# Hybrid conv block on one core: c's row on GpSimd's queue, wide constants for the clock, two unsplit chunks in the lead, and the second half's sum in front of the last chunk

## The chip, the cores and the metric

The kernel runs on one core of one Trainium2 chip. The metric is the device time of one execution in microseconds (us). TensorE is PE in the profile, VectorE is DVE, ScalarE is ACT, GpSimd is POOL and SyncE is SP. All arithmetic is float32; a matmul operand marked fp32r passes through TensorE once, and the kernel reaches float32 accuracy by splitting each operand into a high and a low fp32r part.

## The reference, cut to what matters

```python
def reference(x, c, ...):            # x (1, 1024, 1024), c (1, 1024), all float32
    mod = silu(c) @ w_ada + b_ada    # 6 * 1024 values
    sh1, sc1, g1, sh2, sc2, g2 = split(mod, 6)
    h = rms_norm(x, norm_mix_g) * (1 + sc1) + sh1
    proj = h @ w_in                  # 7 * 1024 columns
    b_s, c_s, v_s, v_c, gl_c, gate_br = split(proj)
    y_a = (b_s * causal_dwconv(c_s * v_s, 3 taps)) @ w_short_out
    u = causal_dwconv(v_c * sigmoid(gl_c), 31 taps) + bias
    y_b = silu(layer_norm(u)) @ w_conf_out
    g_a, g_b = split(sigmoid(gate_br))
    x = x + g1 * ((g_a * y_a + g_b * y_b) @ w_o)
    h2 = rms_norm(x, norm_ffn_g) * (1 + sc2) + sh2
    a, b = split(h2 @ w_ffn_in)
    x = x + g2 * ((silu(a) * b) @ w_ffn_out)
    return rms_norm(x, final_norm_g)
```

## The kernel before

Everything lies transposed: channels on the 128 partitions, positions along the row. The 1024 channels are eight chunks, numbered k = 0 to 7 here as in the code (the words "chunk 8" of the change's title mean k = 7). The 1024 positions are two halves of 512, h = 0 and h = 1. A tile framework fixes the order of the instructions on each engine when the program is built; every engine, and every DMA queue, then goes through its list in order and waits where an operand is not there. `tc.issue_after(ins)` puts what follows behind the instruction `ins` in that planning.

The change is in the lead, the first 5% of the program, up to the second half's first products. Its steps, with lines of the kernel before:

- **c's row.** `c` (4 KB, one partition) is loaded into `crow`, tile name `diff` (L540, issued by ACT), then `vecs` (184 KB of small vectors, L541, issued by ACT). A dummy Silu (L543) loads ACT's table, `crow` goes through Silu (L550), a second dummy (L424) loads the table with the reciprocal root. Two matmuls `cb` (L556) with one row of ones spread silu(c) over all partitions, and ACT copies them to SBUF as `cs` (L562).
- **Clock matmuls.** `keep_clock` (L529 to L536) issues matmuls that nobody reads, 128x128 in float32, chained to the work around them: 7 ahead of `cb`, 2 after each of five additions of squares, 6 on ones after the sum, 10 that read the tile `rx0r`. The tuple `CLOCK` holds these counts.
- **The norm of the first half.** `squares_x` (L488 on ACT, L492 on DVE) squares the eight chunks and adds them, six into one tile and two into another. `norm_start` sums over the partitions with two matmuls `ss` (L502) and takes the reciprocal root on ACT (`rx0r`, L399). `rstd_square` squares that (`rx0t`, L412). `rstd_negative` (L417, L418) is one Newton step on DVE, the second instruction written in place over `rx0r`.
- **The modulation.** For each k two blocks of `w_ada` (512 KB each, tile `ada`) are loaded by SP and multiplied and summed with `cs` on DVE (L329). `affine` (L335) makes the scale, `modulate` (L428 on DVE, L432 or L436 and L440 on ACT, L437 on DVE) makes the operand.
- **The lead's products.** `row_blocks` runs over k and, for each k, over seven output tiles `lead`. For k below `WHOLE` (3) weight and operand go to TensorE unsplit, as float32 (L344, two records for each matmul in the profile). From there on both are split: the weight by ACT (L220, `wh`) and DVE (L221, `wl`), the operand by L436 and L437, and each output tile takes three fp32r matmuls (L348, L349, L351).
- **The norm of the second half.** At k = 5 eight loads of `xT` (256 KB each, L595) are issued, at k = 6 their squares are summed and `ss` and the reciprocal root `rx1` begin, at k = 7 the Newton step ends. Then `row_blocks` runs again for h = 1, beginning with the kept weights of chunks 5, 6 and 7.

Behind the lead come the rest of the input projection, the convolutions, the output projections and the feed-forward part; the change does not touch their code.

Of the kernel before, what the change touches and what calls it, by code (L numbers as in the profile page):

```python
# [44 lines left out]
KC = D // P  # L45
# [4 lines left out]
EPS = 1e-6  # L50
# [3 lines left out]
V_GMIX, V_GFFN, V_GFIN, V_LNG, V_LNB, V_CB = (8 * i for i in range(6))  # L54
# [9 lines left out]


LEAD = 7
WHOLE = 3

CLOCK = (7, 2, 6, 10)


KEPT = 3
SECOND = [*range(KC - KEPT, KC), *range(KC - KEPT)]


SQ_LAST = 2


X1_AT = 5
# [40 lines left out]
def block_kernel(ctx: ExitStack, tc: tile.TileContext, x0, xT, c, vecs, ada, w_first, w_plain, w_duals,  # L122
                 w_short, w_conf, w_o, w_fi, w_fo, w_last, outT):
    nc = tc.nc
# [13 lines left out]
    cp = pool("const", 1)  # L138
# [16 lines left out]
    def ps2_tile(name):  # L155
        return ps2p.tile([P, H], F32, tag="ps2", name=name)
# [30 lines left out]
    ng = cp.tile([P, V_LNG], F32, name="ng")  # L187
# [152 lines left out]
    def mm3(outs, wsl, w, xs, first, last, again=False):  # L340

        if w[1] is None:
            for ps, x in zip(outs, xs):
                mm3.ins = nc.tensor.matmul(ps, w[0][:, wsl], x, start=first, stop=last).ins  # L344
            return
        wh, wl = w[0][:, wsl], w[1][:, wsl]
        for ps, (xh, xl) in zip(outs, xs):
            nc.tensor.matmul(ps, wh, xh, start=first, stop=False, skip_group_check=again)  # L348
# [60 lines left out]
    def rstd_square(begun):  # L409

        ss, eps, r, q, _ = begun
        nc.scalar.activation(q, r, AF.Square, scale=0.5 ** 0.5)  # L412
        return ss, r, q

    def rstd_negative(ss, r, q):

        nc.vector.scalar_tensor_tensor(out=q, in0=ss, scalar=EPS, in1=q, op0=ALU.add, op1=ALU.mult)  # L417
        nc.vector.scalar_tensor_tensor(out=r, in0=q, scalar=1.5, in1=r, op0=ALU.subtract, op1=ALU.mult)  # L418
        return r

    def load_rsqrt(ins):

        with tc.issue_after(ins):
            nc.scalar.activation(cp.tile([P, 1], F32, name="rs"), ones[:, :1], AF.Abs_reciprocal_sqrt)  # L424

    def modulate(src, r, scale, shift, name, begun=None):

# [36 lines left out]
    def row_blocks(act, n, name, ops, unit, joined=2):  # L464


        outs = [(ps_tile if o < 6 else ps2_tile)(f"{name}{o}") for o in range(n)]
        ops = list(ops)
        for k in range(KC):
            if k == len(ops):  # L470
                xs = act(k)
                ops.append((unit(k), xs))
            if KC - joined <= k < KC - 1:
                continue
            for o in range(n):
                for kk in range(KC - joined, KC) if k == KC - 1 else (k,):
                    w, xs = ops[kk]
                    mm3([outs[o]], slice(o * P, o * P + P), w, [xs], kk == 0, kk == KC - 1)
        return outs


    x = {}

    def squares_x(src, acc=None, clock=0):

        for t in src:
            sq = g_tile("sq")
            act = nc.scalar.activation(sq, t, AF.Square, scale=1.0 / 32.0)  # L488
            if acc is None:
                acc = sq  # L490
            else:
                add = nc.vector.tensor_tensor(acc, acc, sq, ALU.add)  # L492
                if clock:
                    keep_clock(keep_clock.ins, clock, sq)
        squares_x.ins = act.ins, add.ins
        return acc

    def norm_start(acc, name, n=H, tile_of=g_tile, ss_tile=ps_tile):
        ss = ss_tile("ss")
        acc = acc if isinstance(acc, list) else [acc]  # L500
        for t in acc:
            norm_start.ins = nc.tensor.matmul(ss[:, :n], ones, t, start=t is acc[0], stop=t is acc[-1]).ins  # L502
        return rstd_start(ss, eps1, name, n, tile_of)
# [22 lines left out]
        nc.scalar.activation(sig, ps, AF.Sigmoid)  # L526
        nc.scalar.dma_start(gate_dram[b, j][:, halves[h]], sig)

    def keep_clock(ins, n, src=None):  # L529

        t = ps2_tile("clock")[:, :P]
        src = ones if src is None else src[:, :P]
        for _ in range(n):
            with tc.issue_after(ins) if ins else ExitStack():
                ins = nc.tensor.matmul(t, ones, src, start=True, stop=True).ins
# [4 lines left out]
    nc.scalar.dma_start(crow, c)  # L540
    nc.scalar.dma_start(vec, vecs)  # L541
    nc.vector.tensor_scalar(ng, vec[:, :V_LNG], -1.0, None, ALU.mult)
    nc.scalar.activation(cp.tile([P, 1], F32, name="si"), ones[:, :1], AF.Silu)  # L543
    xin = {}
    for k in range(0, KC, 2):
        t = uc_tile("x0", T)
        nc.sync.dma_start(t, x0[k // 2])
        xin[k], xin[k + 1] = (t[:, s] for s in halves)
    keep_clock(None, CLOCK[0])
    silu = nc.scalar.activation(crow, crow, AF.Silu)  # L550
    load_rsqrt(silu.ins)
    cb = []
    for s in halves:
        cb.append(ps_tile("cb"))
        with tc.issue_after(keep_clock.ins):
            mm = nc.tensor.matmul(cb[-1], ones[:1], crow[:, s], start=True, stop=True)  # L556
    keep_clock.ins = mm.ins
    acc = squares_x([xin[k] for k in range(KC - SQ_LAST)], clock=CLOCK[1])
    acc = [acc, squares_x([xin[k] for k in range(KC - SQ_LAST, KC)])]
    with tc.issue_after(squares_x.ins[0]):  # L560
        for s, t in zip(halves, cb):
            nc.scalar.copy(cs[:, s], t)  # L562
    with tc.issue_after(keep_clock.ins):
        rx_0 = norm_start(acc, "rx0")
    keep_clock(norm_start.ins, CLOCK[2])
    keep_clock(keep_clock.ins, CLOCK[3], rx_0[2])
    rx_0 = rstd_square(rx_0)

    def lead_w(k):
# [4 lines left out]
            kept.append(w)  # L574
        return w

    def act_x(k, h):
        nonlocal rx_0, rx_1
        if h == 0:
            with ExitStack() as after:  # L580
                after.enter_context(tc.issue_after(modulate.ins[0] if k else squares_x.ins[1]))
                for i in range(2 * k, 2 * k + 2):
                    modulation(i, ucp.tile([P, T + CK - 1], F32, tag="uc", name="ada")[:, :D])
            affine(naff1, k, 8, ng, V_GMIX)
            if k == 0:
                rx_0 = rstd_negative(*rx_0)
            x[k, 0] = s_tile(f"x{k}0")
        whole = h == 0 and k < WHOLE
        hT[k][h] = modulate(x[k, h], rx_1 if h else rx_0, naff1[:, k : k + 1], modc(k),
                            None if whole else f"h{k}{h}", None if h else xin[k])  # L590
        if h == 0:
            if k == X1_AT:
                for i in range(KC):
                    x[i, 1] = s_tile(f"x{i}1")
                    nc.sync.dma_start(x[i, 1], xT[i, :, halves[1]])  # L595
            elif k == X1_AT + 1:
                with tc.issue_after(modulate.ins[2]):
                    rx_1 = squares_x([x[i, 1] for i in range(KC)])
                with tc.issue_after(mm3.ins), tc.issue_after(modulate.ins[1]):
                    rx_1 = rstd_square(norm_start(rx_1, "rx1", ss_tile=ps2_tile))  # L600
            elif k == KC - 1:
                with tc.issue_after(modulate.ins[2]):
                    rx_1 = rstd_negative(*rx_1)
            if whole:
                return x[k, 0]
        elif k < WHOLE:
            hT[k][0] = split(x[k, 0], hl_tile, f"h{k}0")
        return hT[k][h]
# [605 lines left out]
    ss = ps_tile("ss")  # L1214
# [54 lines left out]
    n = 2 * GROUP * P  # L1269
# [184 lines left out]
```

## Time and profile before

| | |
|---|---|
| median of 3 runs | 1476.24 us (1476.24 to 1478.43) |
| the profiled execution, its own time | 1477.93 us |
| its span, first to last instruction | 1476.2 us |
| PE busy | 1462.0 us (99% of the span) |
| DVE busy | 1177.7 us (80%) |
| ACT busy | 617.0 us (42%) |
| POOL busy | 513.3 us (35%) |

The profile is that of one execution, whose own time is 1.7 us above the median of the runs and above its span. Busy times are averages over the whole program; in the first 20 us TensorE mostly runs the clock matmuls, so its busy share says nothing there, and times have to be read from the order of the rows. A row of the timeline gives start, duration, engine, line, operation, tile written and tiles read, and in brackets the idle time of that engine ahead of it with what ended it.

### The profile page before, as it was taken

The numbers are of one execution on the slowest core, as the hardware profiler recorded it, in microseconds if no ns is written. First come the engines' busy times: TensorE is split into PE (matmuls) and PEld (weight loads), VectorE is DVE, ScalarE is ACT, GpSimd is POOL, SyncE is SP. The second block draws the span as 40 slices with busy tenths as digits, with TensorE's granted clock in tenths as the row PEclk, the third lists the DMA queues.
The fourth block names the chain that finished last, engine by engine and source line by source line (L and its number), as shares of the span: only waits on it lengthen the run. The fifth ranks groups of instructions, "written<-read, shape, count | busy, mean of one in ns | idle before, by whom it ended". The sixth has DMA issues, their size and how long they took to land.

```text
span 1476.2 us, 17809 instructions
## 1 busy us (share of the span) xinstructions
PE 1462.0 (99%) x6475; PEld 1200.4 (81%) x6475; DVE 1177.7 (80%) x1623; ACT 617.0 (42%) x896; POOL 513.3 (35%) x459
## 2 busy tenths in 40 slices
PE   9999999999999999999999999999999999999997
PEld 5888888888888888878888878888888888888887
DVE  7999888887998969999687699777777765677755
ACT  4653433333333335555235465444444443222235
POOL 0036677767877771111022001101111015535005
PEclk9999999999999999999999999999999999999999
DMA  8522213222222267376685337655455449988403
GB/s 342 188 64 72 100 58 128 72 86 100 91 67 86 82 219 285 105 237 213 200 311 172 117 100 235 209 176 168 150 192 166 146 149 371 357 287 276 156 1 115
DMA packets 83274, 245.36 MB, mean 166 GB/s; under 512 B 9585, under 2 KB 11761, under 8 KB 83186
## 3 DMA queue, kind: packets, MB, share of 16 engines
q1 hardware_dynamic: 42352, 136.01, 27.6%
q0 software_dynamic: 36944, 95.44, 19.6%
q10 hardware_dynamic: 3890, 12.78, 2.3%
q8 instruction: 51, 0.84, 0.2%
q14 instruction: 37, 0.30, 0.1%
HBM read 181.79 MB, written 62.39 MB: 165 GB/s over the span
## 4 chain that ended last, share of the span: by engine, by line
PE 91%; DVE 6%; DMA 1%; issue 1%; ACT 1%; POOL 0%; POOLq 0%; DVEq 0%; ACTq 0%
PE bank L351 11%; PE bank L348 11%; PE bank L349 11%; PE x L351 7%; PE x L348 7%; PE x L349 7%; PE z L349 4%; PE z L348 4%; PE z L351 4%; PE y L349 3%; PE y L348 3%; PE y L351 3%; PE yb L351 2%; PE yb L348 2%; PE yb L349 2%; PE mix L349 2%
## 5 line engine op out<-in xcount | busy, mean ns | idle before, releaser
L220 ACT CAST wh<-raw 128x1024 fp32r<-128x1024 f32 (+2 forms) x254 | 256.3, 1011 | 485.2 <-PE bank L349 133.6
L221 POOL TENSOR_TENSOR wl<-raw,wh 128x1024 fp32r<-128x1024 f32 x84 | 204.5, 2444 | 81.8 <-ACT wh L220 81.8
L221 DVE TENSOR_TENSOR wl<-raw,wh 128x1024 fp32r<-128x1024 f32 (+2 forms) x170 | 195.0, 1147 | 47.5 <-ACT wh L220 46.2
L838 DVE SCALAR_TENSOR_TENSOR c<-diff,vec,c 128x512 f32<-128x512 f32 x232 | 171.0, 753 | 4.4
L1170 POOL DMA_DIRECT2D hid<-stage x71 | 37.8, 533 | 347.0 <-DVE stage L389 341.0
L348 PE MATMUL bank<-th,wh 128*128 128x512 f32 x288 | 112.0, 389 | 0.0
L349 PE MATMUL bank<-tl,wh 128*128 128x512 f32 x288 | 112.0, 389 | 0.0
L351 PE MATMUL bank<-th,wl 128*128 128x512 f32 x288 | 112.0, 389 | 0.0
L838 DVE SCALAR_TENSOR_TENSOR c<-u,wsum,c 128x512 f32<-128x512 f32 x112 | 84.3, 753 | 2.6
L240 POOL TENSOR_TENSOR raw<-raw 128x1024 f32<-128x1024 f32 x12 | 29.2, 2430 | 130.4 <-DVE wl L221 92.8
L388 ACT CAST stage<-g 128x512 fp32r<-128x512 f32 x62 | 38.4, 622 | 65.9 <-DMA hid<-stage 35.4
L351 PEld LDWEIGHTS bank<-th,wl 128*128 128x128 f32 x288 | 54.1, 188 | 11.3
L349 PEld LDWEIGHTS bank<-tl,wh 128*128 128x128 f32 x288 | 54.1, 188 | 11.2
L348 PEld LDWEIGHTS bank<-th,wh 128*128 128x128 f32 x288 | 54.1, 188 | 11.2
L389 DVE TENSOR_TENSOR stage<-g,stage 128x512 fp32r<-128x512 f32 x62 | 42.4, 689 | 25.3 <-ACT stage L388 25.3
L1196 POOL DMA_DIRECT2D th<-hid x71 | 38.0, 535 | 53.2 <-PE x L351 31.9
L348 PE MATMUL x<-th,wh 128*128 128x512 f32 x144 | 56.1, 390 | 0.0
L349 PE MATMUL x<-tl,wh 128*128 128x512 f32 x144 | 56.0, 389 | 0.0
L351 PE MATMUL x<-th,wl 128*128 128x512 f32 x144 | 56.0, 389 | 0.0
L348 PE MATMUL yb<-zsh,wh 128*128 128x512 f32 x128 | 49.8, 389 | 0.0
L349 PE MATMUL yb<-zsl,wh 128*128 128x512 f32 x128 | 49.8, 389 | 0.0
L351 PE MATMUL yb<-zsh,wl 128*128 128x512 f32 x128 | 49.8, 389 | 0.0
(798 smaller groups left out, 4211.3 us busy)
## 6 DMA issues: line engine op xcount, KB each, us to landing
hid<-stage POOLq DMA_DIRECT2D x71, 512.0 KB, 4.4
raw<-in_w_fi SPq DMA_DIRECT2D x51, 512.0 KB, 3.7
raw<-in_w_duals SPq DMA_DIRECT2D x48, 512.0 KB, 3.5
th<-hid POOLq DMA_DIRECT2D x71, 256.0 KB, 5.7
tl<-hid POOLq DMA_DIRECT2D x71, 256.0 KB, 5.7
ada<-in_ada SPq DMA_DIRECT2D x24, 512.0 KB, 5.9
raw<-in_ada SPq DMA_DIRECT2D x24, 512.0 KB, 4.6
raw<-in_w_fo SPq DMA_DIRECT2D x24, 384.0 KB, 5.7
```

Source lines behind the costliest of these rows:

```text
L220: hi = nc.scalar.copy(wh, raw)
L221: lo = lo_engine.tensor_tensor(wl, raw, f32(wh), ALU.subtract)
L240: eng.tensor_tensor(a["s1"], a["21"], a["22"], ALU.add)
L348: nc.tensor.matmul(ps, wh, xh, start=first, stop=False, skip_group_check=again)
L349: nc.tensor.matmul(ps, wh, xl, start=False, stop=False, skip_group_check=again)
L351: mm3.ins = nc.tensor.matmul(ps, wl, xh, start=False, stop=last, skip_group_check=again).ins
L388: t_split.act = nc.scalar.copy(hi, src).ins
L389: t_split.ins = nc.vector.tensor_tensor(lo, src, f32(hi), ALU.subtract).ins
L838: tap.ins = nc.vector.scalar_tensor_tensor(out=out, in0=src[:, s : s + H], scalar=wt, in1=acc, op0=ALU.mult, op1=ALU.add).ins
L1170: nc.gpsimd.dma_start(hid_dram[key], s)
L1196: nc.gpsimd.dma_start(t, hid_dram[key][:, s])
```

## The change

- `WHOLE` goes from 3 to 2: chunk k = 2 of the first half is split like the later ones.
- `c` is loaded by GpSimd's queue instead of ACT's. ACT's first instructions are then the load of `vecs`, the dummy Silu, Silu of c's row and the second table.
- `keep_clock` can issue wide matmuls: 128x512, fp32r, on a new tile `ones_r` filled by DVE. There are 6 wide ones ahead of `cb`; one small and one wide after each of five additions; 6 wide after the sum; one small on the new tile `newton` and 3 wide; one small on `rx0r` and 2 wide.
- The first Newton instruction writes `newton` and no longer `rx0t`; the second still writes `rx0r`, which no clock matmul reads ahead of it any more.
- The squares of the first half take buffers of the large pool (58) instead of one with 6.
- The first half of `cs` is copied by DVE ahead of the additions, the second by ACT behind the squares. The scaled gains `ng` are made after that copy.
- For k = 7 the modulation's DVE work stands behind the last addition of the second half's squares, and every product of k = 7 stands behind that half's `ss` matmul.

In the program as it is built, this changes the order on the engines in the lead only (up to about 75 us of the profile before); behind it the lists of all engines hold the same instructions in the same order, but for one place in the numbering of GpSimd's DMAs.

```diff
-WHOLE = 3
+WHOLE = 2
-CLOCK = (7, 2, 6, 10)
+CLOCK = (6, range(1, 6), 6, (3, 2))
...
-    def rstd_negative(ss, r, q):
+    def rstd_negative(ss, r, q, t=None):
-        nc.vector.scalar_tensor_tensor(out=q, in0=ss, scalar=EPS, in1=q, op0=ALU.add, op1=ALU.mult)
-        nc.vector.scalar_tensor_tensor(out=r, in0=q, scalar=1.5, in1=r, op0=ALU.subtract, op1=ALU.mult)
+        t = q if t is None else t
+        nc.vector.scalar_tensor_tensor(out=t, in0=ss, scalar=EPS, in1=q, op0=ALU.add, op1=ALU.mult)
+        nc.vector.scalar_tensor_tensor(out=r, in0=t, scalar=1.5, in1=r, op0=ALU.subtract, op1=ALU.mult)
...
         for k in range(KC):
             if k == len(ops):
                 xs = act(k)
                 ops.append((unit(k), xs))
+                first = getattr(act, "first", None)
...
-                    mm3([outs[o]], slice(o * P, o * P + P), w, [xs], kk == 0, kk == KC - 1)
+                    with tc.issue_after(first) if first and k == KC - 1 else ExitStack():
+                        mm3([outs[o]], slice(o * P, o * P + P), w, [xs], kk == 0, kk == KC - 1)
...
-                if clock:
-                    keep_clock(keep_clock.ins, clock, sq)
+                if i in clock:
+                    keep_clock(keep_clock.ins, 1, sq)
+                    keep_clock(keep_clock.ins, 1, wide=True)
...
-    def keep_clock(ins, n, src=None):
-        t = ps2_tile("clock")[:, :P]
-        src = ones if src is None else src[:, :P]
+    def keep_clock(ins, n, src=None, wide=False):
+        t = ps2_tile("clock")
+        lhs, src = (ones_r[:, :P], ones_r) if wide else (ones, ones if src is None else src[:, :P])
         for _ in range(n):
             with tc.issue_after(ins) if ins else ExitStack():
-                ins = nc.tensor.matmul(t, ones, src, start=True, stop=True).ins
+                ins = nc.tensor.matmul(t[:, : src.shape[-1]], lhs, src, start=True, stop=True).ins
...
-    nc.scalar.dma_start(crow, c)
+    nc.gpsimd.dma_start(crow, c)
     nc.scalar.dma_start(vec, vecs)
-    nc.vector.tensor_scalar(ng, vec[:, :V_LNG], -1.0, None, ALU.mult)
...
-    keep_clock(None, CLOCK[0])
+    ones_r = s_tile("ones_r", F32R)
+    nc.vector.memset(f32(ones_r), 1.0)
+    keep_clock(None, CLOCK[0], wide=True)
...
-    acc = squares_x([xin[k] for k in range(KC - SQ_LAST)], clock=CLOCK[1])
-    acc = [acc, squares_x([xin[k] for k in range(KC - SQ_LAST, KC)])]
+    copy = nc.vector.tensor_copy(cs[:, halves[0]], cb[0])
+    with tc.issue_after(copy.ins), tc.issue_after(load_rsqrt.ins):
+        nc.vector.tensor_scalar(ng, vec[:, :V_LNG], -1.0, None, ALU.mult)
+        acc = squares_x([xin[k] for k in range(KC - SQ_LAST)], clock=CLOCK[1], tile_of=s_tile)
+        acc = [acc, squares_x([xin[k] for k in range(KC - SQ_LAST, KC)], tile_of=s_tile)]
     with tc.issue_after(squares_x.ins[0]):
-        for s, t in zip(halves, cb):
-            nc.scalar.copy(cs[:, s], t)
+        nc.scalar.copy(cs[:, halves[1]], cb[1])
     with tc.issue_after(keep_clock.ins):
         rx_0 = norm_start(acc, "rx0")
-    keep_clock(norm_start.ins, CLOCK[2])
-    keep_clock(keep_clock.ins, CLOCK[3], rx_0[2])
+    keep_clock(norm_start.ins, CLOCK[2], wide=True)
...
-                after.enter_context(tc.issue_after(modulate.ins[0] if k else squares_x.ins[1]))
+                after.enter_context(tc.issue_after(squares_x.ins[1] if k in (0, X1_AT + 2) else modulate.ins[0]))
...
             if k == 0:
-                rx_0 = rstd_negative(*rx_0)
+                t = s_tile("newton")
+                rx_0 = rstd_negative(*rx_0, t)
+                for src, n in zip((t, rx_0), CLOCK[3]):
+                    keep_clock(keep_clock.ins, 1, src)
+                    keep_clock(keep_clock.ins, n, wide=True)
...
-                with tc.issue_after(modulate.ins[2]):
+                with tc.issue_after(modulate.ins[2]), tc.issue_after(modulate.ins[1]):
                     rx_1 = squares_x([x[i, 1] for i in range(KC)])
                 with tc.issue_after(mm3.ins), tc.issue_after(modulate.ins[1]):
                     rx_1 = rstd_square(norm_start(rx_1, "rx1", ss_tile=ps2_tile))
+                act_x.first = norm_start.ins
...
-        lead = row_blocks(lambda i: act_x(SECOND[i] if h else i, h), LEAD, "lead", ops, again_w if h else lead_w, 1 + h)
+        lead = row_blocks(act_x if h == 0 else lambda i: act_x(SECOND[i], 1), LEAD, "lead", ops,
+                          again_w if h else lead_w, 1 + h)
```

More of the change, by code (lines that the diff above doesn't have):

```diff
@@ L423, in load_rsqrt @@
         with tc.issue_after(ins):
-            nc.scalar.activation(cp.tile([P, 1], F32, name="rs"), ones[:, :1], AF.Abs_reciprocal_sqrt)
+            act = nc.scalar.activation(cp.tile([P, 1], F32, name="rs"), ones[:, :1], AF.Abs_reciprocal_sqrt)
+        load_rsqrt.ins = act.ins
     def modulate(src, r, scale, shift, name, begun=None):
@@ L467, in row_blocks @@
         outs = [(ps_tile if o < 6 else ps2_tile)(f"{name}{o}") for o in range(n)]
-        ops = list(ops)
+        ops, first = list(ops), None
         for k in range(KC):
@@ L477, in row_blocks, with squares_x @@
                     w, xs = ops[kk]
-                    mm3([outs[o]], slice(o * P, o * P + P), w, [xs], kk == 0, kk == KC - 1)
+                    with tc.issue_after(first) if first and k == KC - 1 else ExitStack():
+                        mm3([outs[o]], slice(o * P, o * P + P), w, [xs], kk == 0, kk == KC - 1)
         return outs
     x = {}
-    def squares_x(src, acc=None, clock=0):
-        for t in src:
-            sq = g_tile("sq")
+    def squares_x(src, acc=None, clock=(), tile_of=g_tile):
+        for i, t in enumerate(src):
+            sq = tile_of("sq")
             act = nc.scalar.activation(sq, t, AF.Square, scale=1.0 / 32.0)
@@ L555, in block_kernel @@
         with tc.issue_after(keep_clock.ins):
-            mm = nc.tensor.matmul(cb[-1], ones[:1], crow[:, s], start=True, stop=True)
-    keep_clock.ins = mm.ins
-    acc = squares_x([xin[k] for k in range(KC - SQ_LAST)], clock=CLOCK[1])
-    acc = [acc, squares_x([xin[k] for k in range(KC - SQ_LAST, KC)])]
+            keep_clock.ins = nc.tensor.matmul(cb[-1], ones[:1], crow[:, s], start=True, stop=True).ins
+    copy = nc.vector.tensor_copy(cs[:, halves[0]], cb[0])
[3 more added lines that the diff above has]
+        acc = [acc, squares_x([xin[k] for k in range(KC - SQ_LAST, KC)], tile_of=s_tile)]
     with tc.issue_after(squares_x.ins[0]):
-        for s, t in zip(halves, cb):
-            nc.scalar.copy(cs[:, s], t)
+        nc.scalar.copy(cs[:, halves[1]], cb[1])
     with tc.issue_after(keep_clock.ins):
         rx_0 = norm_start(acc, "rx0")
-    keep_clock(norm_start.ins, CLOCK[2])
-    keep_clock(keep_clock.ins, CLOCK[3], rx_0[2])
+    keep_clock(norm_start.ins, CLOCK[2], wide=True)
     rx_0 = rstd_square(rx_0)
@@ L575, in lead_w, with act_x @@
         return w
-    def act_x(k, h):
+    def act_x(k, h=0):
         nonlocal rx_0, rx_1
```

## The prediction, as it was put on record

> **What bounds the kernel now.** I read the page first, then the chain of work that ended last in order of time, then the timelines of PE, DVE and ACT for the first 75 us.
>
> ```profile
> span 1476.2 us, 17809 instructions
> PE 1462.0 (99%) x6475; PEld 1200.4 (81%) x6475; DVE 1177.7 (80%) x1623; ACT 617.0 (42%) x896; POOL 513.3 (35%) x459
> ```
>
> ```profile
> 1.06 3.35 PE clock L535 x14
> 4.42 3.71 PE cb L556 x4
> 8.12 4.34 PE clock L535 x20
> 12.47 1.72 PE ss L502 x4
> 14.19 3.58 PE clock L535 x32
> 17.79 0.70 DVE rx0r L418
> 18.52 0.76 DVE x L428
> 19.31 0.73 ACT x L432
> 20.08 18.29 PE lead L344 x42
> ```
>
> TensorE is busy all the time; its longest pause is the one ahead of the first real product at 20.08, from the end of the clock matmuls (14.19 + 3.58 = 17.77) on, 2.3 us. From there on it is fed, so whatever brings the first product forward, or takes matmuls out of the stream, shortens the whole; behind the lead the instruction lists are the same and the shift is carried to the end. Ahead of 20.08 the chain runs over clock matmuls, that is, TensorE's own queue sets the time of the sums that DVE and ACT wait for.
>
> The rows also show TensorE slow and then fast: the same 128x128 matmul record takes 4.34 / 20 = 0.217 us from 8.12 on and 3.58 / 32 = 0.112 us from 14.19 on. The change is between those two stretches; I take 0.217 as cold and 0.112 as warm.
>
> **The change part by part.** The sum is made against the profiled execution, 1477.93 us with a span of 1476.2, and then taken off the median, 1476.24, which lies 1.7 us lower; the three runs reach from 1476.24 to 1478.43. About 0.2% (2.95 us) is what a measurement of this kernel can tell from no change.
>
> *c's row.*
>
> ```profile
> 0.74 0.51 ACTq L540 DMA_DIRECT2D diff<-in_c  x1
> 0.74 0.30 POOL L173 MEMSET fill<- 128x248 f32 x1 [0.29 <-POOLq L1443]
> ...
> 3.09 1.04 ACT L550 ACTIVATE diff<-diff 1x1024 f32<-1x1024 f32 x1
> ```
>
> c's row had landed by 3.09, when Silu began behind the load of its table. Without the issue of 0.51 on ACT's queue the table comes 0.5 earlier and Silu could start at 2.6. But c now goes behind GpSimd's fill, issued at 0.74 + 0.30 = 1.05, through a queue whose first landing the trace of before does not show. Three rows bound it, by the DMAs' times to landing: ACT's gate stores, GpSimd's `hid` stores, and `vec`, which shared the engines with x's loads as c will.
>
> ```profile
> DMA to landing us min/median/max: 2.0/2.0/2.9
> ```
>
> ```profile
> DMA to landing us min/median/max: 2.9/4.4/8.3
> ```
>
> ```profile
> vec<-in_vecs ACTq DMA_DIRECT2D x1, 184.0 KB, 5.0
> ```
>
> So c lands between 1.05 + 2.0 = 3.05 and 1.05 + 5.0 = 6.05. I take 3.1: the first row is of 256 KB, the second of 512 KB, and c has 4 KB. Silu then ends at 4.1 to 4.2, as before. The six wide clock matmuls wait for DVE to fill `ones_r` (about 1.5) and take, cold, twice the fp32r pitch of 0.228 us (a split chunk below: 4.78 for 21), 6 x 0.456 = 2.7, so they end at 4.2. `cb` starts at 4.3, where it was 4.42: 0.1 gained, 3 us lost at the other bound.
>
> *Clock matmuls up to `ss`.* `cb` takes 3.71 and ends at 8.0. Before, 20 records took 4.34. Now there are five pairs, each two cold small records and a cold wide one: 5 x (2 x 0.217 + 0.456) = 4.5. The additions that release them come in time: DVE's copy of `cs` follows the first `cb` (half of 3.71, at 6.2), the additions run from about 7.1. So `ss` starts at 12.5, where it was 12.47. The squares no longer wait for buffers, and `cs` is half done early, but both hide behind TensorE's queue: at nothing. If TensorE is warm earlier, that cover is gone and they count (below).
>
> *From `ss` to the first product.*
>
> ```profile
> 15.60 0.69 DVE L417 SCALAR_TENSOR_TENSOR rx0t<-ss,rx0t 128x512 f32<-128x512 f32 x1 [1.25 <-ACT rx0t L412]
> 17.79 0.69 DVE L418 SCALAR_TENSOR_TENSOR rx0r<-rx0t,rx0r 128x512 f32<-128x512 f32 x1 [1.50 <-PE clock L535]
> ```
>
> The second Newton instruction waited 1.50 for the clock matmuls that read the tile it overwrites. That wait goes: the new clock matmuls read `newton`, and `rx0r` only behind the write. What is late next is the first Newton instruction itself, bound by ACT (1.25 idle). The modulation's sum for k = 0, which was done ahead of that idle time, ends no later than before. The clock matmuls behind (6 wide, then 2 + 3, then 2 + 2, 0.11 to 0.23 each) are done well ahead of the operand. So the first product comes 1.5 earlier, plus 0.1 from `cb`: at 18.5. Gain 1.6.
>
> *Chunk k = 2 split.*
>
> ```profile
> 52.52 0.39 PE L348 MATMUL lead<-h60h,wh 128*128 128x512 f32 x1
> ...
> 58.17 0.39 PE L348 MATMUL lead<-h70h,wh 128*128 128x512 f32 x1
> ...
> 62.95 0.39 PE L348 MATMUL lead<-h51h,wh 128*128 128x512 f32 x1
> ```
>
> A whole chunk takes 18.29 / 3 = 6.10. Chunks 3 to 5 take (52.52 - 38.37) / 3 = 4.72, chunk 7 4.78. So 1.35 goes out of TensorE's stream. It costs DVE a `wl` and a low operand more, 4.93 a chunk instead of 3.27:
>
> ```profile
> 21.79 0.75 DVE L428 SCALAR_TENSOR_TENSOR x<-x,naff,rx0r 128x512 f32<-128x512 f32 x1
> ...
> 28.33 0.75 DVE L428 SCALAR_TENSOR_TENSOR x<-x,naff,rx0r 128x512 f32<-128x512 f32 x1
> ...
> 33.26 0.75 DVE L428 SCALAR_TENSOR_TENSOR x<-x,naff,rx0r 128x512 f32<-128x512 f32 x1
> ```
>
> (18.52 to 21.79 is 3.27, 28.33 to 33.26 is 4.93.) With the first modulation at 17.0, that of k = 2 comes at 23.5 and its operands at 25.4; TensorE asks for them at 18.5 + 12.2 = 30.7. k = 6 is ready at 23.5 + 4 x 4.93 + 1.8 = 45.0 and wanted at 18.5 + 12.2 + 4 x 4.72 = 49.6. DVE stays ahead; without that lead the edit would cost what it is short.
>
> *The second half's sum.* `ss` lay within chunk 6 and now stands behind it, ahead of every product of k = 7. On ACT the built order is now: `wh` of k = 7, `rx1r`, `rx1t`, then `h70h`. Before, `h70h` came ahead of `rx1r`:
>
> ```profile
> 14.22 0.69 ACT L399 ACTIVATE rx0r<-ss,eps 128x512 f32<-128x512 f32 x1 [2.47 <-PE ss L502]
> 14.94 0.63 ACT L412 ACTIVATE rx0t<-rx0r 128x512 f32<-128x512 f32 x1
> ...
> 54.59 0.73 ACT L436 ACTIVATE h70h<-x,mod 128x512 fp32r<-128x512 f32 x1 [3.61 <-DVE x L428]
> 56.76 0.69 ACT L399 ACTIVATE rx1r<-ss,eps 128x512 f32<-128x512 f32 x1 [1.45 <-PE ss L502]
> 57.95 0.62 ACT L412 ACTIVATE rx1t<-rx1r 128x512 f32<-128x512 f32 x1
> ```
>
> ```profile
> 55.86 0.86 PE ss L502 x2
> ```
>
> ```profile
> 5.55 3.21 ACT L488 ACTIVATE sq<-x 128x512 f32<-128x512 f32 x6
> ```
>
> So the first product of k = 7 waits for `h70h`, `h70h` is queued behind `rx1r`, and `rx1r` waits for `ss`, the last thing ahead on TensorE. TensorE then idles for 0.04 (56.72 to 56.76), 0.72 (14.22 to 14.94), 0.62, 0.73 and 0.04 (19.31 + 0.73 to 20.08): 2.15 us that it did not idle before. The additions do not hold `ss` up: k = 6 is done on DVE at 45, eight squares of 3.21 / 6 = 0.535 end on ACT at 49.4, the last addition at 50.1, and TensorE gets to `ss` at 18.5 + 12.2 + 18.9 + 4.8 = 54.4. DVE's work for k = 7 behind the additions (two sums, the scale, the modulation, `wl`: about 4.4) ends at 54.5, ahead of `h70h` at 57.3. One block of `w_ada` is now queued on SP ahead of the eight `xT` loads; it waits for a buffer that DVE frees in chunk 4, at about 31.8 by the pace above, no later than those loads began before:
>
> ```profile
> 32.77 6.81 SPq L595 DMA_DIRECT2D x<-in_xT  x8
> ```
>
> Chunk 7 then runs from 57.3 to 62.1. The second half's first low operand comes at about 62.2 (two Newton steps, three modulations and one more from 58.0), so 0 to 0.3 more; I take 0.1.
>
> **Sum:** 1.6 + 1.35 - 2.15 - 0.1 = 0.7 us gained: 62.2 in place of 62.95 at the second half's first product. 1477.93 becomes 1477.2, and the median 1475.5.
>
> **The rivals.**
>
> *Warm early.* If the wide matmuls bring TensorE to the warm pitch ahead of the five pairs, these take half, and DVE and the squares set `ss`. From 5.4 eight squares at 0.535 end at 9.7. DVE's additions, from 7.1 and no faster than the squares, end at 11.0 (about 0.65 each); `ss` ends at 12.6, Newton starts at 14.0 (1.4 behind, as 14.19 to 15.60), the first product comes 3.0 later at 17.0. Gain 3.1 + 1.35 - 2.25 = 2.2: 1474.0, and 1473.3 if `cb` is warm too. For it: 512 columns without a pause. Against it: the trace stays cold from 1.06 to past 8.12 with TensorE hardly idle, and the first wide stretch is only 2.7 us, shorter than the 3.35 that did not suffice. The Trainium skill ("TensorE: Matmul & The Clock Gate", "What's actually happening") has the clock rise after about 3.4 us of sustained activity, in windows that run free of the kernel's start. By that rule the whole stretch from 1.06 should have been warm by 8; the 0.217 us at 8.12 disagree, unless one-row `cb` matmuls do not count as activity. Chance 0.2.
>
> *c late, slower.* If c lands as `vec` did, 5.0 us behind its issue, Silu runs from 6.05 to 7.1, `cb` starts at 7.2, and everything in this cold chain moves by 2.9: 0.7 - 2.9 = -2.2, 1478.4. It decides from the point where c lands later than 3.1 + 0.7 = 3.8; slower by 0.2% needs 6.8. For it: x's 2 MB are queued first; against it: c has one small piece. Chance 0.15.
>
> *The stall is hidden.* If `h70h` finds ACT free, the 2.15 are not paid: 1473.3. The order of ACT's list speaks against it. Chance 0.05.
>
> **How the numbers follow.** My forecast, 1475.5, has 0.6; its own range is 1474.3 to 1476.9, as the moment of warming can move `ss` by a microsecond either way. The range 1473.4 to 1478.2 reaches into the rivals on both sides. Faster by over 0.2% (below 1473.3) needs the early warmth whole or the hidden stall: 0.12. Slower by over 0.2%: 0.07. Within: 0.81.
>
> **What would show it.** Right: `cb` at 4.3, the second Newton instruction straight behind the first, first product near 18.5, about 6.1 us for each of two whole chunks, a PE wait of about 2.1 us on ACT's `h70h`, `h51h` products near 62.2. Wrong: clock records at 0.112 us ahead of 8 us; Silu later than 4; no wait ahead of k = 7; waits of TensorE on DVE for k = 2 to 6; or a time below 1473.3 or above 1479.2.

## The result, and the profile after

The changed kernel takes 1481.84 us (median of 7 runs, 1481.1 to 1482.87) where the kernel before, run beside it, takes 1477.35 (7 runs, 1476.24 to 1480.24): a ratio of 1.0027, 95% interval 1.0015 to 1.0038. It is slower by 4.5 us. Forecast were 0.7 gained and a median of 1475.5, with a range up to 1478.2. The kernel before stood at 1476.24 when the forecast was made and 1.1 higher beside the changed one; so of the 6.3 us between forecast and result, 5.2 belong to the change.

The page's head, and the chain of work that ended last in order of time (start, duration, what), of the kernel after:

```profile
span 1480.0 us, 17766 instructions
...
PE 1461.2 (99%) x6452; PEld 1199.3 (81%) x6452; DVE 1179.9 (80%) x1626; ACT 616.6 (42%) x896; POOL 514.9 (35%) x460
```

```profile
1.31 5.58 DMA diff<-in_c
6.91 1.06 ACT diff L556
8.02 3.78 PE cb L562 x4
11.79 4.80 PE clock L540 x15
16.60 2.41 PE ss L507 x4
...
20.41 0.70 DVE newton L418
21.14 0.70 DVE rx0r L419
...
23.43 12.28 PE lead L344 x28
...
59.54 0.87 PE ss L507 x2
60.43 0.70 ACT rx1r L399
61.15 0.63 ACT rx1t L412
61.78 0.62 ACT h70h L438
62.45 1.43 PE lead L348 x5
```

The chain no longer begins on TensorE. Its first long piece is a DMA: c's 4 KB, on GpSimd's queue, land 5.58 behind their issue at 1.31, at 6.89, where before they had landed by 3.09. Everything in the cold start hangs behind that. PE's busy share is 99% in both kernels; only the order of the rows shows the loss. The two longest waits of PE in the first 120 us (what it waited for: us in all, times, longest):

```profile
PE cb L562 <- ACT diff L556: 3.5, 1, 3.5
PE lead L348 <- ACT h70h L438: 2.0, 1, 2.0
```

The first is new, and in the forecast it stood only as a rival; the second is the stall ahead of k = 7 that was forecast. By rows: `cb` starts at 8.02 in place of 4.42 before (3.60 later), the first product at 23.43 in place of 20.08 (3.35 later), and the second half's first product, on `h51h`, follows 43.9 behind that, at 67.34 in place of 62.95 (4.39 later). The medians differ by 4.49, the spans of the two profiled executions by 3.8.

### The profile page after: what moved, and what is told of

The parts are those of the page before. It is cut to its first block, busy times and chain, and to the rows that moved or that the text cites. A ratio compares the mean times of both kernels' runs of the same rounds, so it can differ in the third digit from the quotient of the medians.

```text
span 1480.0 us, 17766 instructions
## 1 busy us (share of the span) xinstructions
PE 1461.2 (99%) x6452; PEld 1199.3 (81%) x6452; DVE 1179.9 (80%) x1626; ACT 616.6 (42%) x896; POOL 514.9 (35%) x460
## 4 chain that ended last, share of the span: by engine, by line
PE 91%; DVE 5%; ACT 1%; issue 1%; DMA 1%; POOL 0%; POOLq 0%; DVEq 0%; ACTq 0%
PE bank L351 11%; PE bank L349 11%; PE bank L348 11%; PE x L351 7%; PE x L348 7%; PE x L349 7%; PE z L348 4%; PE z L351 4%; PE z L349 4%; PE y L351 3%; PE y L349 3%; PE y L348 3%; PE yb L348 2%; PE yb L349 2%; PE yb L351 2%; PE mix L348 2%
## 5 line engine op out<-in xcount | busy, mean ns | idle before, releaser
L240 DVE TENSOR_TENSOR raw<-raw 128x1024 f32<-128x1024 f32 (+1 forms) x17 | 19.2, 1130 | 40.7 <-DMA raw<-in_w_fi 30.9
```

The source lines that it names most:

```text
L240: eng.tensor_tensor(a["s1"], a["21"], a["22"], ALU.add)
```

## The experiments

Two questions. First, is c's queue the whole loss, and if so, what holds a 4-KB load for 5.6 us: GpSimd's queue as such, or x's loads on the same DMA engines? Second, are the other steps of the sum worth what they were put at? A ratio is against the kernel before, run on the same chip beside it; for two kernels there is a single execution and its profile, and no interval.

**c back on ACT's queue, all else as changed.**

```diff
-    nc.gpsimd.dma_start(crow, c)
+    nc.scalar.dma_start(crow, c)
```

> The changed kernel with c's row loaded by ACT's queue again, nothing else. Theory (c lands late through GpSimd's queue, 6.9 us in the trace, and the cold chain behind it moves with it): Silu of c's row starts near 3.1 in place of 6.91, the spreading matmuls near 4.4 in place of 8.02, the first product near 19.7 in place of 23.43, and the time falls by 3.7 us from 1481.8 to about 1478.1. Rival (the wide clock matmuls, the copy of cs on DVE and the squares' buffers cost the time, c only waits along): the first product moves by less than 1 us and the time stays above 1481.

Measured: 1477.55 (11 runs), ratio 1.0004 (0.9995 to 1.0013). The chain of this kernel:

```profile
1.62 2.93 PE clock L540 x6
4.55 3.71 PE cb L562 x4
8.26 4.80 PE clock L540 x15
13.06 2.12 PE ss L507 x4
...
19.60 12.28 PE lead L344 x28
```

This one line takes back some 4 us (the change as a whole is 4.5 above the kernel before, this one 0.5), and the chain begins on TensorE again. The first product comes at 19.60, 0.48 ahead of the kernel before.

**The kernel before, with c on GpSimd's queue and nothing else.**

```diff
-    nc.scalar.dma_start(crow, c)
+    nc.gpsimd.dma_start(crow, c)
```

> The kernel before with c's row loaded by GpSimd's queue, nothing else. Theory (the queue alone delays c): c lands near 6.9 us, the spreading matmuls start near 8.0 in place of 4.34, the first product near 23.7 in place of 20.08, and the time rises by 3.7 us over the kernel before, to about 1481. Rival (c is late in the changed kernel because of something else there, such as the fill of the wide constants on DVE while GpSimd writes its descriptors, or ACT's earlier load of vecs): c lands before 4 us and the time rises by less than 1 us.

Measured: 1481.29 (5 runs), ratio 1.0032 (1.0020 to 1.0045). The chain of this kernel:

```profile
1.31 5.44 DMA diff<-in_c
...
7.88 3.77 PE cb L556 x4
```

The queue alone makes the whole loss, in either kernel. DVE's fill of the wide constants, which might have disturbed GpSimd's issue, is not in this one. The rest of the change comes, in sum, to about nothing.

**What holds c: x's loads kept back until c has landed.** c stays on GpSimd's queue; a copy of one element of c into each of x's tiles makes SP's loads wait for c.

```diff
         t = uc_tile("x0", T)
+        nc.vector.tensor_copy(t[:1, :1], crow[:1, :1])
-        nc.sync.dma_start(t, x0[k // 2])
+        load.hold = nc.sync.dma_start(t, x0[k // 2]).ins
...
-        nc.sync.dma_start(raw, src)
+        with tc.issue_after(load.hold):
+            nc.sync.dma_start(raw, src)
```

> The changed kernel with the four loads of x, and all of SP's loads behind them, held until c's row has landed through GpSimd's queue. Theory A (c waits because its queue shares the DMA engines with x's 2 MB): without them c lands as later GpSimd transfers began, within about 2 us of its issue at 1.3, so near 3.3. Theory B (the first transfer of GpSimd's queue is late by itself, whatever else moves): c lands near 6.5 to 6.9 all the same. The time as a whole means nothing here, since x comes late.

Measured: 1477.67 (one execution). The chain of this kernel, and its DMA issues (tile, queue, count, KB each, us to landing) beside those of the kernel after:

```profile
1.30 2.16 DMA diff<-in_c
...
4.95 3.78 PE cb L564 x4
```

```profile
x<-in_x SPq DMA_DIRECT2D x4, 512.0 KB, 4.8
...
diff<-in_c POOLq DMA_DIRECT2D x1, 4.0 KB, 2.2
```

```profile
x<-in_x SPq DMA_DIRECT2D x4, 512.0 KB, 5.8
...
diff<-in_c POOLq DMA_DIRECT2D x1, 4.0 KB, 5.6
```

The same issue by GpSimd lands in 2.2 us when x's 2 MB are not queued, and in 5.6, beside x's own 5.8, when they are. It is the company, not the software queue by itself. The Trainium skill ("DMA: Bandwidth & Descriptors", "Anatomy of one DMA — SWDGE (gpsimd) path") fits about 2.0 us plus the bytes to a DMA by GpSimd; the 2.2 agree, the 5.6 do not: the fit has no term for x's loads on the same engines.

The packets that the DMA engines moved tell how far c waits. By queue (packets, MB, share of the engines' time), for the kernel after, from 1 to 5.3 us and then from 5.3 to 6.2:

```profile
q1 hardware_dynamic: 235, 0.90, 69.4%
q10 hardware_dynamic: 144, 0.19, 11.9%
```

```profile
q1 hardware_dynamic: 98, 0.34, 98.3%
q0 software_dynamic: 32, 0.00, 3.0%
```

q1 is SP's queue, q10 ACT's and q0 GpSimd's. All 32 packets of c (16 of 256 bytes, and 16 of 4 that close them) move between 5.3 and 6.2, when 0.90 MB of x's 2 MB are through. In this trace the packets that close x's second load fall at 5.49 to 6.16, and those that close c's at 5.49 to 6.16 too; with x held back c's packets begin at 2.71. So c waits for the first two of x's four loads.

**c on ACT's queue, but behind `vec`.**

```diff
-    nc.gpsimd.dma_start(crow, c)
     nc.scalar.dma_start(vec, vecs)
+    nc.scalar.dma_start(crow, c)
```

> The changed kernel with c's row on ACT's queue behind vec (184 KB), where it was ahead of vec before. Theory A (any queue that joins x's loads late waits for them): c lands 4 to 5 us behind its issue at about 1.2, as vec did, so near 5.5 to 6, and the first product comes near 22.5. Theory B (GpSimd's queue alone is late): c lands within 2 us of its issue, near 3, Silu runs from about 3.1, and the first product is where it is with c ahead of vec, near 19.6.

Measured: 1479.48 (one execution). The chain of this kernel:

```profile
1.18 3.83 DMA diff<-in_c
...
6.14 3.78 PE cb L562 x4
```

A hardware queue does not save c either, if it comes behind others: 3.83 us. Issued at 0.74 by ACT, in the kernel before, c had landed by 3.09: its one packet of 4 KB moved at 1.79, together with the first of x's. Here it is issued at 1.18, behind `vec` in the same queue, and its packet moves at 4.36, among the last of `vec`'s (2.30 to 4.61). So this kernel shows a wait in c's own queue; c late and alone on a hardware queue was not tried. The Trainium skill ("DMA: Bandwidth & Descriptors", "Queues, rings and completion order") has each engine take the descriptors of one queue in order, and go round its queues by packets, each a group of descriptors that it drains before it turns to the next queue. The place behind `vec` agrees. Why c on a queue of its own waits for two of x's loads, and not for one turn, that rule alone does not give; how many descriptors of x made one such group, no view here shows.

**The order of k = 7 taken out, all else as changed.** The three places that put the second half's `ss` ahead of k = 7 are undone (c stays on GpSimd's queue).

```diff
-                act_x.first = norm_start.ins
...
-                after.enter_context(tc.issue_after(squares_x.ins[1] if k in (0, X1_AT + 2) else modulate.ins[0]))
+                after.enter_context(tc.issue_after(modulate.ins[0] if k else squares_x.ins[1]))
...
-                with tc.issue_after(modulate.ins[2]), tc.issue_after(modulate.ins[1]):
+                with tc.issue_after(modulate.ins[2]):
```

> The changed kernel without the last part of the change: chunk k = 7's modulation and products no longer stand behind the second half's sum, so h70h comes ahead of rx1r on ACT again, and the ss matmul lies within chunk 7 as built. Theory A (the wait of 2.05 us on h70h is a cost of that order alone): it goes, nothing takes its place, 1481.8 - 2.05 = 1479.8. Theory B (with TensorE's stream shortened by the split of k = 2 the chain from the second half's sum to its first operand is late either way, and the order only chooses the place of the wait): no wait ahead of k = 7, but about 2 us at the second half's first product h51h, and the time stays at 1481.8.

Measured: 1481.86 (6 runs), ratio 1.0032 (1.0020 to 1.0044): no different from the change as a whole. PE's waits, and the chain there, of this kernel:

```profile
PE lead L348 <- ACT h51h L438: 1.9, 1, 1.9
```

```profile
60.91 0.87 PE ss L507 x2
...
63.18 1.28 ACT L526
64.47 1.08 ACT sig L526 x2
65.56 0.62 ACT h51h L438
66.22 1.45 PE lead L348 x5
```

The stall ahead of k = 7 is gone, and one of the same size stands behind it: with two unsplit chunks the planner slides `ss` into k = 7, and the reciprocal root, 1.28 at L526 (as long as each load of a table on ACT) and the sigmoids come ahead of `h51h`. The added order decides where TensorE waits, not how long. That the two times are equal is in part chance: by rows `h51h` starts 1.12 ahead of the kernel after (66.22, 67.34), 0.91 of it already at the first product (c landed 0.35 sooner, `ss` is 0.56 shorter), and a stretch at half clock behind the wait (last section) takes that away again.

**`WHOLE` at 2 in the kernel before, and nothing else.**

```diff
-WHOLE = 3
+WHOLE = 2
```

> The kernel before with WHOLE at 2 and nothing else: chunk k = 2 is split. Theory A (the step of the prediction stands by itself): TensorE's stream in the lead is 1.35 shorter, k = 7 starts at about 56.8, no new waits, the median falls by 1.35, to about 1475.8. Rival B (the chain behind the second half's sum has less slack than 1.35): the last addition (it ends at 55.1 before, or later by what a wl and a low operand more cost DVE) holds ss, or the second half's first operand h51l holds TensorE; a new wait of 0.5 to 1.3 and 0 to 0.8 gained. By B the order given to k = 7 in the change would be an answer to that.

Measured: 1478.96 (11 runs), ratio 1.0013 (1.0003 to 1.0024): slower by 1.3, so neither expectation held: the wait comes at the second half's first operand, as the second had it, but it is longer. The longest wait of PE behind the first product, and the chain of this kernel:

```profile
PE lead L348 <- ACT h51h L436: 1.9, 1, 1.9
```

```profile
58.61 0.87 PE ss L502 x2
```

The split does take its 1.35 out of the stream, and then the same slide of `ss` (58.61, where before had 55.86) gives it back with a wait of 1.9. The last addition ends at 56.52, 2.1 ahead of `ss`, so it is not DVE that holds the sum; it is the place of two matmuls in TensorE's list.

**`ss` inside k = 6.** c on ACT's queue, and the last three output tiles of k = 6 put behind `ss` as well as k = 7, so that TensorE has work while ACT makes the root and `h70h`.

```diff
-                    with tc.issue_after(first) if first and k == KC - 1 else ExitStack():
+                    with tc.issue_after(first) if first and (k == KC - 1 or k == KC - 2 and o >= 4) else ExitStack():
...
-    nc.gpsimd.dma_start(crow, c)
+    nc.scalar.dma_start(crow, c)
```

> The changed kernel with c's row on ACT's queue and with the second half's sum put in front of the last three output tiles of chunk k = 6 (and still in front of k = 7). Theory (the chain from the sum to h70h is hidden if the sum starts while TensorE still has products of k = 6): the additions end before TensorE gets there, the wait ahead of k = 7 falls from 2.05 to about 0.4 us, bound by the modulation of k = 7 on DVE, and the time is 1.6 us below that of the run that only moves c, about 1476.5. Rival (the wait moves to DVE's additions, which are not done when TensorE reaches the sum): TensorE waits within k = 6 instead and nothing is gained, 1478.1.

Measured: 1476.14 (11 runs), ratio 0.9994 (0.9986 to 1.0003), 1.4 below the same kernel without the three tiles. The waits of PE and the chain of this kernel:

```profile
PE lead L348 <- ACT h70h L438: 0.2, 1, 0.2
```

```profile
8.25 4.50 PE clock L540 x15
12.75 1.73 PE ss L507 x4
```

The wait falls from 2.1 to 0.2, and by the medians three quarters of that reach the end, though the intervals of the two kernels overlap. By rows `h51h` begins 2.5 earlier (61.00, 63.52), of which 0.7 is an earlier warming ahead of the first product.

**c as the first load of SP's queue.** To the kernel just above: c ahead of x on SP's queue, and four wide clock matmuls ahead of `cb` in place of six.

```diff
-CLOCK = (6, range(1, 6), 6, (3, 2))
+CLOCK = (4, range(1, 6), 6, (3, 2))
...
-    nc.scalar.dma_start(crow, c)
+    nc.sync.dma_start(crow, c)
```

> The run with the second half's sum within k = 6, but with c's row as the first load of SP's queue, ahead of x, and 4 wide clock matmuls ahead of the spreading ones in place of 6. ACT then issues one load less, as in the changed kernel. Theory: Silu runs at about 2.6 in place of 3.1, the spreading matmuls start at 3.8 in place of 4.5, and since TensorE's cold queue sets the time up to the second stage, the first product comes 0.7 us earlier and the time falls by 0.7 to about 1475.4. Rival (x's loads, now 0.45 us later, or the additions set the time): no gain against 1476.1.

Measured: 1475.55 (11 runs), ratio 0.9988 (0.9979 to 0.9997). `cb` starts at 3.70 in place of 4.54, and the first `ss` at 11.95 in place of 12.75. First in the queue, c is early. But TensorE now waits 0.4 on DVE's `h70l`, k = 7 takes 5.57 in place of 4.90, and `h51h` begins at 61.00 in both kernels. The medians are 0.6 apart, the intervals overlap, and the two profiled executions took the same time (1475.25 and 1475.26): that anything of the 0.8 reaches the end is not shown.

**`cb` over 128 rows.** To the kernel with `ss` inside k = 6: silu(c) goes into the first row of a tile whose other rows are zero, and the two `cb` matmuls use all 128 rows. The arithmetic is the same.

```diff
-    silu = nc.scalar.activation(crow, crow, AF.Silu)
+    z = [s_tile(f"z{h}") for h in range(2)]
+    for h, s in enumerate(halves):
+        nc.vector.memset(z[h], 0.0)
+    for h, s in enumerate(halves):
+        silu = nc.scalar.activation(z[h][:1], crow[:, s], AF.Silu)
...
-            keep_clock.ins = nc.tensor.matmul(cb[-1], ones[:1], crow[:, s], start=True, stop=True).ins
+            keep_clock.ins = nc.tensor.matmul(cb[-1], ones, z[h], start=True, stop=True).ins
```

> The run with the second half's sum within k = 6 (c on ACT's queue, 6 wide clock matmuls), but silu(c) lies in the first row of a 128-row operand whose other rows are zero, so that the two spreading matmuls use all 128 rows; same result. Theory A (the clock's monitor does not count one-row matmuls as activity, so that the stretch from 1.6 us never fills a window): TensorE turns warm between 5 and 8.5 us in place of 12, the additions set ss, the first product comes near 17 in place of 18.8, and the time falls by 1.5 to 2 us, to about 1474.4. Theory B (rows do not matter): TensorE turns warm at 11.5 to 15 as before and the time stays at 1476.1.

Measured: 1473.91 (10 runs), ratio 0.9978 (0.9968 to 0.9988), the best of all. The profiled execution, 1475.99, is the slowest of the ten; a pause of 1.9 ahead of one product at 1266.4 us, which no other trace here has, is most of its distance from the median. The timeline of PE in the kernel with one-row `cb` matmuls, and then in this one:

```profile
8.63 0.77 PE L540 MATMUL clock<-ones_r 128*128 128x512 f32 x1
```

```profile
4.35 2.87 PE L566 MATMUL cb<-z,ones 128*128 128x512 f32 x4
...
7.19 0.47 PE L540 MATMUL clock<-ones_r 128*128 128x512 f32 x1
...
11.05 1.98 PE L507 MATMUL ss<-sq,ones 128*128 128x512 f32 x4 [0.95 <-DVE sq L496]
```

The clock matmuls behind `cb` are warm already (a wide one takes 0.47, not 0.77), `cb` itself takes 2.87 and not 3.71 (4.54 to 8.25 in the other kernel), and `ss` waits for DVE's additions rather than for TensorE's own queue. In the one-row kernel TensorE is no less busy up to there, and stays cold: one-row matmuls keep the engine busy in the profile without bringing the clock up. The trace's records of the granted clock, which begin where it comes up, say the same: 12.27 with one row, 6.33 with 128. (The windows of the profile print 1.00 ahead of the first record; that TensorE is cold there is seen by the length of its records.) By rows the first product and `h51h` come 1.4 earlier than in the one-row kernel; the medians are 2.2 apart.

**The 128-row `cb` alone, in the kernel before.** The same edit, nothing else.

> The kernel before with nothing changed but the two cb matmuls: c's row lies in the first of 128 rows, the other rows are zero, and the matmul uses all rows. Same arithmetic. Theory A (one-row matmuls do not count as work for the clock): full clock at about 6 to 7 instead of 12.1; the clock records behind cb take 0.112 instead of 0.217, so that the additions on DVE set the time of ss (last one ends at 11.6, or a little earlier): ss ends at about 12.6 instead of 14.2, and the first product comes 1.5 earlier, at 18.6; the median falls by 1.5, to about 1475.6. Rival B (the 128-row matmuls helped the changed kernel only because its clock matmuls are wide): the clock stays low past 8, and the time is within 0.5 of before's.

Measured: 1477.30 (11 runs), ratio 0.9994 (0.9985 to 1.0003). The chain of this kernel, and windows of it and of the kernel before (stretch, its length, busy time and count of PE, PEld, DVE, ACT and POOL, granted clock, DMA share, GB/s):

```profile
10.75 1.98 PE ss L502 x4
...
18.63 19.86 PE lead L344 x42
```

```profile
18.60:20.60 2.00, 1.97 (x3) 0.94 (x4) 1.96 (x6) 0.00 (x0) 0.00 (x0) 0.50 0.40 70
20.60:22.00 1.40, 1.40 (x3) 0.57 (x2) 1.40 (x2) 0.72 (x1) 0.00 (x0) 0.56 0.84 319
```

```profile
20.10:22.00 1.90, 1.90 (x5) 0.94 (x6) 1.86 (x6) 0.00 (x0) 0.00 (x0) 1.00 0.20 28
```

The warm clock comes early here too, and the first product 1.45 earlier, at 18.63 as expected. But behind the 2.3 us of idle ahead of it the granted clock is at 0.50 from 18.41 to 21.82, and three unsplit chunks take 19.86 in place of 18.29. In the kernel before the same idle of 2.3 left the clock at 1.00. The Trainium skill ("TensorE: Matmul & The Clock Gate", "What's actually happening") puts the fall behind an idle window of about 3.4 us, and has these windows run free of the program. A pause of 2.3 us disagrees with an idle time of that length; free-running windows agree with what tells the two kernels apart (last section).

**All together.** To the 128-row version: c first on SP's queue, four wide clock matmuls, the scaled gains behind the additions.

```diff
-CLOCK = (6, range(1, 6), 6, (3, 2))
+CLOCK = (4, range(1, 6), 6, (3, 2))
...
-    nc.scalar.dma_start(crow, c)
+    nc.sync.dma_start(crow, c)
...
-        nc.vector.tensor_scalar(ng, vec[:, :V_LNG], -1.0, None, ALU.mult)
...
+    with tc.issue_after(squares_x.ins[1]):
+        nc.vector.tensor_scalar(ng, vec[:, :V_LNG], -1.0, None, ALU.mult)
```

> The 128-row version of the two cb matmuls (c's row in the first of 128 rows, the others zero; second half's sum within k = 6), with three things more: c is the first load of SP's queue, four wide clock matmuls instead of six ahead of cb, and the scaled gains ng behind the additions of the squares instead of ahead of them. In the 128-row version the chain ran from vec's landing (7.0) over ng and DVE's additions to ss at 11.05, with TensorE waiting 1.0 for them, and DVE set the lead. Theory A (the clock is not what limits the start any more; vec's landing and DVE do): cs is copied 0.6 earlier, the additions start when ACT's second square is there (about 6.3 instead of 7.12), ss at 10.3, the first product at 16.7, and the whole falls 0.7 below the 128-row version's: about 1473.2. Rival B: with c earlier the cb matmuls begin earlier in cold time and the clock comes up no earlier than at 6.3, or DVE's list behind the additions waits for x or w_ada anyway: nothing gained, 1473.9. Slower than 1474.5 would say that x's loads, now behind c, hold the squares.

Measured: 1475.66 (11 runs), ratio 0.9985 (0.9976 to 0.9994), 1.7 above the 128-row version by itself. Two rows of this kernel's timeline:

```profile
5.16 1.13 ACT L492 ACTIVATE sq<-x 128x512 f32<-128x512 f32 x2
...
7.59 3.67 ACT L492 ACTIVATE sq<-x 128x512 f32<-128x512 f32 x6 [1.30 <-DMA x<-in_x]
```

`cb` and the first two squares came earlier, and then the third square waited 1.30 for x. That c's place ahead of x made this wait is not shown: with c first on SP's queue and one-row `cb`, x's loads stand behind c in the same way, their median to landing is 5.1 us (6.4 here), and the first four squares run from 5.02 on without a pause. Nor is it the larger part: against the 128-row version the first product is 0.3 late (17.80, 17.48) and `h51h` 1.1 (60.70, 59.61), and most of the difference is k = 7, 5.58 long in place of 4.94, with the same wait on `h70l` as in the other kernel with c first on SP's queue.

## Why the prediction was wrong, point by point

- **c's row: the failed step.** It said "I take 3.1", and c landed at 6.89. The bounds quoted were 3.05 to 6.05, and the row of a load that shares the engines with x (`vec`, 5.0) was named as the upper one. The choice went to the lower end because c has only 4 KB; that put c below even the shortest landing in the row of GpSimd's own queue (2.9). Size was the wrong criterion: at this place the time to landing is the wait behind x, 5.2 to 5.6 in three kernels, and 2.2 with x held back. The row with the same company was the nearest one.
- **The rival "c late, slower" is what happened.** Its mechanism and its point of decision were right (it needs c later than 6.8 to be slower by 0.2%; c came at 6.89). Its price of 2.9 was 0.8 short, since c is issued at 1.31 and not 1.05 and takes 5.58 and not 5.0; `cb` moved by 3.72 against the forecast 4.3. Its chance of 0.15, and a range that ended at its price, were too small.
- **The five pairs and `ss`: mis-sized.** Put at 4.5 and 1.72, they took 4.80 and 2.41 here, 4.80 and 2.12 with c on ACT's queue, 4.50 and 1.73 with `ss` in k = 6. The spread is the moment of warming (the granted clock came up at 17.83, 13.71 and 12.27), for which a microsecond either way had been allowed. With 3.72 for c, 0.3 and 0.69, and 0.2 in smaller terms, the first product stands at 23.43 and not 18.5.
- **"Warm early" did not come.** All 15 records of the pairs took 4.80, cold, and the warmth came only during `ss`. The reservation that one-row `cb` matmuls might not count as activity was the right one: with 128 rows the early warmth comes, and the median is 2.2 us lower (1476.14 to 1473.91).
- **The Newton wait: right.** The second instruction follows the first without a pause (20.41, 21.14); from the end of `ss` to the first product it is 4.42, where before it was 5.89: 1.47 gained against 1.5.
- **The split of k = 2: right as a term, wrong as a gain by itself.** Two whole chunks take 12.28. But in the kernel before the same edit loses 1.3, as `ss` slides. The sum as written took both, since it also charged the 2.15.
- **The stall ahead of k = 7: right.** 2.05 measured for 2.15, for the reason given (`h70h` behind `rx1r` on ACT). From the first product to `h51h` it took 43.9 for a forecast of 43.7.

Without c's step the forecast would have been 0.7 gained, and the kernel with c on ACT's queue measured 0.5 lost, with an interval from 0.7 gained to 1.9 lost. So the rest of the sum was right to about a microsecond, in the direction of the warming.

## What to carry to other kernels

At the start of a program, price a load by who shares the DMA engines with it, not by its bytes: 4 KB cost 2.2 us without x's loads and 5.6 behind two of them. Issue first what a long dependent chain hangs on, and look at what then comes second: with c first on SP's queue the first product gained 0.8, and a wait on `h70l` took most of that back. When two instructions in another engine's list decide a stall, an order added in one place may only move the stall, as it did here; give the waiting engine independent work there instead, as the three tiles behind `ss` did.

## What the runs showed of the hardware that was not expected

- c's 4 KB needed 3.8 us to landing behind `vec` in ACT's queue, and 5.2 to 5.6 on GpSimd's queue, which held nothing else: there its packets came only with the end of x's second load.
- Matmuls over one row (3.71 us for the four `cb` records) did not bring TensorE's clock up; the same product over 128 rows did. In the ten kernels with one row the granted clock came up 3.9 to 6.0 us behind the end of `cb` (12.09 in the kernel before); in the three with 128 rows it came up at 4.76, 5.74 and 6.33, 3.7 to 4.7 behind the first clock matmul.
- A pause of TensorE of 1.9 to 2.3 us was followed by 3.41 us at a granted clock of 0.50 in two kernels, and by nothing in others with a pause as long (the kernel before, the kernel after). One is the 128-row `cb` alone, above; the other is the kernel without the order of k = 7, where TensorE paused from 64.31 to 66.22 (a window of it, columns as above):

```profile
68.00:71.00 3.00, 3.00 (x9) 2.35 (x8) 3.00 (x5) 1.80 (x3) 0.00 (x0) 0.50 0.25 93
```

Where the pause falls tells the two sorts apart. In each trace the granted clock changes only at whole multiples of 3.413 us from the moment it first came up. Counted in such stretches, the 1.91 us of this pause lie all within 64.14 to 67.56, and the clock fell at 67.56; of the 2.33 in the 128-row `cb` alone 2.11 lie within 15.00 to 18.41, and it fell at 18.41. In the kernel before the 2.3 are halved by a boundary, 1.16 on either side. The most idle stretch without a fall in any of the thirteen traces has 1.80 (the kernel after, of its 2.05). So here the clock fell where 1.9 us or more of one stretch were idle. That is read off two falls; no run moved a pause on purpose.
